# A decoder step on one core: the yo product moved from the first to the last place of each output run, B's transposes moved next to C·Bᵀ

## The chip, the cores and the metric

The kernel runs on one core of one Trainium2 chip, in a single launch. The metric is the device time of one execution in microseconds (us); lower is better.

## The reference

One inference step of a one-layer decoder trunk, for a prompt of 256 tokens and 8 sample requests of 4 tokens each (288 columns together). The core of what the change touches is the second head group of the mixer, a Mamba-2 chunked scan:

```python
proj = h @ lp['w_in']
u_pool, z, xbc, dt_raw = jnp.split(proj, ...)
pool_out = pool_mixer(u_pool, ...)
...
CB = jnp.einsum('bclgn,bcsgn->bclsg', Cm, Bm)
y_diag = jnp.einsum('bclsg,bclsgr,bcsgrp->bclgrp', CB, Lm, xdt)
...
y_off = jnp.einsum('bclgn,bcgrpn,bclgr->bclgrp', Cm, h_starts, jnp.exp(cs))
y = (y_diag + y_off).reshape((b, nc * q) + xdt.shape[3:])[:, :L]
...
y = y + d_skip * xs
y = rmsnorm(y * jax.nn.silu(z), norm_g)
...
mix = jnp.concatenate([pool_out, ssd_out], axis=-1) @ lp['w_out']
x = x + g1 * mix
...
x = x + g2 * ffn_out
```

Widths: model 2048, pooling mixer 512 (4 groups of 128), scan 1536 (24 heads of 64, in 4 groups of 6), state 128. Around it stand adaLN modulation from a 2048 x 12288 weight, RMSNorms and a gated MLP. Inputs and outputs are float32.

## The kernel before

Everything is held transposed: features on 128 partitions, 288 token columns. A large projection splits each float32 weight tile of 128x1024 into a rounded high part and a low part, and adds three products per 128x128 block: high by high, high by low, low by high (`mm3`, L304 to L306). For each such tile, called a half here (two for each block of 128 output rows), SP loads the raw tile (L271), ACT casts it into a `whi` slot (L290) and DVE subtracts into a `wlo` slot (L292). There are two slots of each kind in this stage: the cast of a half waits until TensorE is through with the half before the last.

The stage in question runs from about 236 to 395 us. Its outer loop goes over 16 halves of the `uz` projection (blocks 10 to 15, then 1 and 0; `project_units`). Between the pairs of blocks, a chain of generators (`back`) is pulled one step at a time: the convolution of each scan group (`conv_group`) and the scan itself (`ssd_group`, four groups). After the uz halves come the halves of the out projection (`out_units`), `mm_out` for the scan features and `mm_outp` for the four pooling groups.

One call of `ssd_group(g)` yields these steps: the transposes of x into tokens (`xt`, L788) with `xdt` and `xde` on DVE; the transposes of B (`bt`, L795, copied by ACT at L796); C·Bᵀ (`cb`, L802); the chunk states (`s`, L814, L821) and the product of the 8 sample states with C (`yo`, L834); then three pairs of heads t = 0, 1, 2. For each pair `decays(t)` broadcasts the cumulated decays by matmul (`cse`, L852), makes `e` on ACT (L857 to L859) and multiplies it on DVE with the C·Bᵀ block (`e`, L860) and with C (`ec`, L861). `outputs(t)` adds up the pair's output in one PSUM bank, `y`: six lines of short matmuls of 64 output rows by 128 or 32 columns, and a product with `yo` (L868) of 128 rows by 32 columns for the state part of the samples. DVE then adds the skip (L881) and multiplies with the gate (L885); ACT squares and POOL sums the squares (`ssq`).

Other work stands between these on the same engines. The modulation weights come in visits: four raw tiles of 512 KB into four own slots (`rawa`), 16 short matmuls (L406), and at once the loads of the next visit. The pooling groups (`pool_units`) build windowed sums on DVE (`pp`, `pq`, `pout`) and take one matmul each (L940). After the scan, `ysum` (L242) sums the squares over partitions, ACT and DVE turn the sums into 1/root (L248, L249), and `pbrstdy` (L255) spreads the result. The operand of the out projection is split like a weight, into `mixh` on ACT and `mixl` on DVE (L1127 and L1128, 12 of each).

All engines work in order. The order on each is not written out by hand in this stage. It is made when the program is built: a scheduler takes the instructions in the order written, with priorities for some, and places each when its inputs, its slot and its engine are free by its own cost model. PSUM banks for short-lived results (`aux`) are four, in turn. So a product that is written in another place can move other instructions on every engine.

Of the kernel before, what the change touches and what calls it, by code (L numbers as in the profile page):

```python
# [18 lines left out]
P = 128  # L19
D = 2048  # L20
KT = D // P
NP = 256
NB, NL = 8, 4
NS = NB * NL
N = NP + NS
# [139 lines left out]
def kernel(ctx: ExitStack, tc, ins, outs):  # L165
    nc = tc.nc
# [13 lines left out]
    def aux(name):  # L180
        return px.tile([P, 512], F32, tag="aux", name=name)
# [10 lines left out]
    seli = vec[:, K_SEL:K_SEL + 32]  # L192
# [345 lines left out]
    for q in range(4):  # L538
        t = mx.tile([P, 4, N], F32, tag="blk", name=f"xa{q}", bufs=4)
# [226 lines left out]
    def bc64(ap):  # L766
        return ap.unsqueeze(2).to_broadcast([ap.shape[0], HG, 64])

    def heads(ap):
        return ap.rearrange("p (h q) -> p h q", h=HG)  # L770

    def ssd_group(g):
# [10 lines left out]
        xdt = kp.tile([P, 3, G6], F32, tag="hmod", name=f"xdt{g}", bufs=2)  # L783
        xde = kp.tile([P, 3, G6], F32, tag="hmod", name=f"xde{g}", bufs=2)
        for c in range(3):
# [3 lines left out]
            nc.vector.tensor_tensor(heads(xdt[:, c, :]), heads(pt[:, :G6]), bc64(dt[:, c, hs]), ALU.mult)  # L789
            nc.vector.tensor_tensor(heads(xde[:, c, :]), heads(pt[:, :G6]), bc64(dtr["dtde"][:, c, hs]), ALU.mult)  # L790
        yield
        bt = sx[0].tile([P, 3, P], F32, tag="bt", name=f"bt{g}")
        pt = aux(f"bt{g}")
        for c in range(3):
            nc.tensor.transpose(pt[:, c * P:(c + 1) * P], toks(3, c), ident)  # L795
        nc.scalar.copy(bt.rearrange("p c n -> p (c n)"), pt[:, 0:3 * P])  # L796

        yield
        pcb = aux(f"cb{g}")
        for c in range(3):  # L800
            n = min(P, N - c * P)
# [35 lines left out]
        yo = sx[0].tile([P, G6], F32, tag="yo", name=f"yo{g}")  # L837
# [26 lines left out]
        def outputs(t, e, ec):  # L864
            assert (g, t) in zdone
            pq = aux(f"y{g}_{t}")
            rows = [slice(0, 64), slice(64, P)]
            nc.tensor.matmul(pq[:, NP:N], yo[:, P * t:P * t + P], seli, start=True, stop=False)  # L868
            for i, r in enumerate(rows):
                f = slice(64 * (2 * t + i), 64 * (2 * t + i) + 64)  # L870
                f = slice(64 * (2 * t + i), 64 * (2 * t + i) + 64)
                nc.tensor.matmul(pq[r, NP:N], xdt[:, 2, f], e[:, i, NP:N], start=False, stop=True)
            for i, r in enumerate(rows):
                f = slice(64 * (2 * t + i), 64 * (2 * t + i) + 64)
                nc.tensor.matmul(pq[r, 0:P], xdt[:, 0, f], e[:, i, 0:P], start=True, stop=True)
            for i, r in enumerate(rows):
                f = slice(64 * (2 * t + i), 64 * (2 * t + i) + 64)
                nc.tensor.matmul(pq[r, P:NP], xdt[:, 1, f], e[:, i, P:NP], start=True, stop=False)
                nc.tensor.matmul(pq[r, P:NP], s1[:, f], ec[:, i, :], start=False, stop=True)
            yt = cf[:, t, 0:N]  # L880
            nc.vector.scalar_tensor_tensor(out=yt, in0=yt,  # L881
                                           scalar=vec[:, V_D + 3 * g + t:V_D + 3 * g + t + 1],
                                           in1=pq[:, :N], op0=ALU.mult, op1=ALU.add)
            zt = zy[g][:, t, :]
            nc.vector.tensor_tensor(zt, zt, yt, ALU.mult)  # L885
            sq = kp.tile([P, N], F32, tag="xsq", name=f"ysq{g}_{t}", bufs=2)
            nc.scalar.activation(sq, zt, AF.Square)
            if g + t == 0:
                nc.gpsimd.tensor_copy(ssq, sq)
            else:  # L890
                nc.gpsimd.tensor_tensor(ssq, ssq, sq, ALU.add)
# [4 lines left out]
        yield  # L896
        dec.append(decays(1))
        outputs(0, *dec[0])
        yield
        dec.append(decays(2))  # L900
        outputs(1, *dec[1])
        yield
        outputs(2, *dec[2])
        yield

# [55 lines left out]
    with in_order(*(e.engine for e in (nc.tensor, nc.scalar, nc.vector))):  # L961
# [3 lines left out]
        for q in range(4):  # L965
# [5 lines left out]
            for i in range(4):  # L971
                nc.tensor.matmul(ssum[32 * i:32 * i + 32, :N], ones[:, 0:32], sq[:, i, :],
                                 start=(q == 0), stop=(q == 3), tile_position=(0, 32 * i))
# [54 lines left out]
    def take(gn, n):  # L1028
        for _ in range(n):
            next(gn)  # L1030
            yield

    ssd3 = ssd_group(3)
    back = chain(conv0, h0s(0), zip2(ssd_group(0), conv_group(1)), h0s(1),
                 zip2(ssd_group(1), conv_group(2)), h0s(2), zip2(ssd_group(2), conv_group(3)), h0s(3),
                 zip2(take(ssd3, TK), chain(pool_units(UEARLY[0]), pool_units(UEARLY[1]))))
    credit = {}
# [506 lines left out]
```

## Time and profile before

| what | value |
|---|---|
| time, median of 3 runs | 1345.85 us (1345.23 to 1345.96) |
| the profiled execution | 1344.82 us |
| its span in the trace | 1343.0 us, mean granted TensorE clock 0.998 |
| TensorE weight loads (PEld), busy | 1245.8 us |
| VectorE (DVE) busy | 823.3 us |
| ScalarE (ACT) busy | 578.4 us |
| GpSimd (POOL) busy | 221.3 us |

A line of the profile names the source line, the engine, the operation, the tile written, the tiles read and the shape. "busy" is the time in which an instruction of the engine was in work; matmuls overlap, so the distance between the starts of two matmuls is less than the duration of one. Waits are put down to the instruction that came last. The line numbers are those of the kernel before.

### The profile page before, as it was taken

The numbers are of one execution on the slowest core, as the hardware profiler recorded it, in microseconds if no ns is written. First come the engines' busy times: TensorE is split into PE (matmuls) and PEld (weight loads), VectorE is DVE, ScalarE is ACT, GpSimd is POOL, SyncE is SP. The second block draws the span as 40 slices with busy tenths as digits, with TensorE's granted clock in tenths as the row PEclk, the third lists the DMA queues.
The fourth block names the chain that finished last, engine by engine and source line by source line (L and its number), as shares of the span: only waits on it lengthen the run. The fifth ranks groups of instructions, "written<-read, shape, count | busy, mean of one in ns | idle before, by whom it ended". The sixth has DMA issues, their size and how long they took to land.

```text
span 1343.0 us, 26201 instructions
## 1 busy us (share of the span) xinstructions
PE 1328.6 (99%) x10517; PEld 1245.8 (93%) x10517; DVE 823.3 (61%) x1384; ACT 578.4 (43%) x912; POOL 221.3 (16%) x447
## 2 busy tenths in 40 slices
PE   9999999999999999999999999999999999999997
PEld 7899988776789889989999999999999999999997
DVE  5675569878765478555565455665655556666543
ACT  5343244677733335433433333434433334443442
POOL 0000012123122222102121001222210021122221
PEclk9999999999999999999999999999999999999999
DMA  9999778888898877776455555555555555555541
GB/s 372 405 371 376 275 266 303 312 303 314 299 397 331 309 255 263 277 273 226 169 194 168 169 175 183 204 184 200 185 164 167 186 192 192 193 197 195 179 132 71
DMA packets 97482, 323.19 MB, mean 241 GB/s; under 512 B 10768, under 2 KB 19920, under 8 KB 97360
## 3 DMA queue, kind: packets, MB, share of 16 engines
q1 hardware_dynamic: 93456, 310.72, 65.0%
q0 software_dynamic: 3184, 9.69, 2.0%
q8 instruction: 82, 1.34, 0.4%
q10 hardware_dynamic: 720, 1.11, 0.3%
q14 instruction: 40, 0.33, 0.1%
HBM read 309.78 MB, written 10.39 MB: 238 GB/s over the span
## 4 chain that ended last, share of the span: by engine, by line
PE 94%; DMA 4%; DVE 1%; ACT 0%; issue 0%; SPq 0%; POOL 0%; DVEq 0%
PE mm_down L305 7%; PE mm_down L304 7%; PE mm_down L306 7%; PE mm_val L305 6%; PE mm_gate L304 6%; PE mm_gate L305 6%; PE mm_val L306 6%; PE mm_gate L306 6%; PE mm_val L304 6%; PE xbc L304 4%; PE xbc L305 4%; PE xbc L306 4%; PE adap L406 4%; DMA raw_adap<-wflat 3%; PE adag L373 2%; PE mm_out L304 2%
## 5 line engine op out<-in xcount | busy, mean ns | idle before, releaser
L305 PE MATMUL mm_down<-al,whi_down 128*128 128x288 f32 x688 | 202.5, 294 | 0.0
L304 PE MATMUL mm_down<-ah,whi_down 128*128 128x288 f32 x688 | 202.4, 294 | 0.0
L306 PE MATMUL mm_down<-ah,wlo_down 128*128 128x288 f32 x688 | 202.0, 294 | 0.0
L305 PE MATMUL mm_val<-h2l,whi_val 128*128 128x288 f32 x640 | 189.1, 296 | 0.0
L305 PE MATMUL mm_gate<-h2l,whi_gate 128*128 128x288 f32 x640 | 189.0, 295 | 0.0
L304 PE MATMUL mm_gate<-h2h,whi_gate 128*128 128x288 f32 x640 | 188.7, 295 | 0.0
L306 PE MATMUL mm_val<-h2h,wlo_val 128*128 128x288 f32 x640 | 188.4, 294 | 0.0
L306 PE MATMUL mm_gate<-h2h,wlo_gate 128*128 128x288 f32 x640 | 188.3, 294 | 0.0
L304 PE MATMUL mm_val<-h2h,whi_val 128*128 128x288 f32 x640 | 188.0, 294 | 0.0
L292 DVE TENSOR_TENSOR wlo_gate<-raw_gate,whi_gate 128x1024 fp32r<-128x1024 f32 x80 | 98.6, 1232 | 132.7 <-ACT whi_gate L290 130.5
L292 DVE TENSOR_TENSOR wlo_down<-raw_down,whi_down 128x1024 fp32r<-128x1024 f32 x96 | 108.1, 1126 | 116.8 <-ACT whi_down L290 115.9
L290 ACT CAST whi_down<-raw_down 128x1024 fp32r<-128x1024 f32 x96 | 92.4, 962 | 166.8 <-PE mm_down L305 119.2
L290 ACT CAST whi_gate<-raw_gate 128x1024 fp32r<-128x1024 f32 x80 | 84.0, 1051 | 158.2 <-PE mm_gate L305 75.9
L290 ACT CAST whi_val<-raw_val 128x1024 fp32r<-128x1024 f32 x80 | 84.1, 1051 | 128.3 <-issue 113.6
L304 PE MATMUL xbc<-h1h,whi_xbc 128*128 128x288 f32 x448 | 133.1, 300 | 0.8 <-ACT h1h L491 0.7
L305 PE MATMUL xbc<-h1l,whi_xbc 128*128 128x288 f32 x448 | 132.3, 296 | 0.0
L306 PE MATMUL xbc<-h1h,wlo_xbc 128*128 128x288 f32 x448 | 130.1, 295 | 0.0
L304 PEld LDWEIGHTS mm_down<-ah,whi_down 128*128 128x128 f32 x688 | 129.2, 188 | 0.0
L305 PEld LDWEIGHTS mm_down<-al,whi_down 128*128 128x128 f32 x688 | 129.1, 188 | 0.0
L306 PEld LDWEIGHTS mm_down<-ah,wlo_down 128*128 128x128 f32 x688 | 129.0, 188 | 0.0
L304 PEld LDWEIGHTS mm_gate<-h2h,whi_gate 128*128 128x128 f32 x640 | 120.3, 188 | 5.0 <-ACT ah L1307 4.2
L306 PEld LDWEIGHTS mm_gate<-h2h,wlo_gate 128*128 128x128 f32 x640 | 120.5, 188 | 0.0
(335 smaller groups left out, 2978.5 us busy)
## 6 DMA issues: line engine op xcount, KB each, us to landing
raw_adap<-wflat SPq DMA_DIRECT2D x128, 512.0 KB, 6.2
raw_gate<-wflat SPq DMA_DIRECT2D x80, 512.0 KB, 3.6
raw_val<-wflat SPq DMA_DIRECT2D x80, 512.0 KB, 3.5
raw_ada<-wflat SPq DMA_DIRECT2D x64, 512.0 KB, 9.6
raw_xbc<-wflat SPq DMA_DIRECT2D x50, 512.0 KB, 9.7
raw_down<-wflat SPq DMA_DIRECT2D x48, 512.0 KB, 3.5
raw_out<-wflat SPq DMA_DIRECT2D x32, 512.0 KB, 7.4
raw_down<-wflat SPq DMA_DIRECT2D x32, 384.0 KB, 3.6
```

Of the source, the lines that this page charges most:

```text
L290: yield nc.scalar.copy(hi[:, :n], raw[:, a:a + n])
L292: yield hi, lo, nc.vector.tensor_tensor(lo[:, :n], raw[:, a:a + n], hi[:, :n].bitcast(F32), ALU.subtract)
L304: nc.tensor.matmul(ps, whi[:, w], bh, start=first, stop=False)
L305: nc.tensor.matmul(ps, whi[:, w], bl, start=False, stop=False)
L306: nc.tensor.matmul(ps, wlo[:, w], bh, start=False, stop=last)
L373: i = nc.tensor.matmul(ps[32 * j:32 * j + 32, :nb], sc_c[:, ck, :], raw[:, c:c + nb], start=q0 + n == 0, stop=q0 + AQ[gi] >= nq and n + 1 ...
L406: i = nc.tensor.matmul(ps[32 * j:32 * j + 32, :], sc_c[:, k, :], raw[:, 512 * (j % 2):512 * (j % 2) + 512], start=not begun and k == step - 1,
```

## The change

It moves two things within `ssd_group` and adds no instruction: TensorE has 9152 rows before and after (a row can stand for several equal instructions).

```diff
         yield
+        yield
         bt = sx[0].tile([P, 3, P], F32, tag="bt", name=f"bt{g}")
         pt = aux(f"bt{g}")
         for c in range(3):
             nc.tensor.transpose(pt[:, c * P:(c + 1) * P], toks(3, c), ident)
         nc.scalar.copy(bt.rearrange("p c n -> p (c n)"), pt[:, 0:3 * P])
-
-        yield
         pcb = aux(f"cb{g}")
...
             pq = aux(f"y{g}_{t}")
             rows = [slice(0, 64), slice(64, P)]
-            nc.tensor.matmul(pq[:, NP:N], yo[:, P * t:P * t + P], seli, start=True, stop=False)
-            for i, r in enumerate(rows):
...
-                nc.tensor.matmul(pq[r, NP:N], xdt[:, 2, f], e[:, i, NP:N], start=False, stop=True)
             for i, r in enumerate(rows):
                 f = slice(64 * (2 * t + i), 64 * (2 * t + i) + 64)
                 nc.tensor.matmul(pq[r, 0:P], xdt[:, 0, f], e[:, i, 0:P], start=True, stop=True)
...
+            for i, r in enumerate(rows):
+                f = slice(64 * (2 * t + i), 64 * (2 * t + i) + 64)
+                nc.tensor.matmul(pq[r, NP:N], xdt[:, 2, f], e[:, i, NP:N], start=True, stop=False)
+            nc.tensor.matmul(pq[:, NP:N], yo[:, P * t:P * t + P], seli, start=False, stop=True)
```

In the orders below, line numbers of the changed kernel are one or two lower or a few higher than those of the kernel before. The first place is group 1. On TensorE the yo products of its pairs 1 and 2 stood before among the matmuls of uz, far ahead of the runs to which they belong:

```order
L306 MATMUL mm_uz_12_3531<-h1h12_130,wlo_uz_12_1_3648 128x288
L304 MATMUL mm_uz_12_3531<-h1h13_131,whi_uz_12_1_3646 128x288
L868 MATMUL y1_1_3629<-vec_70,yo1_3484 128x32
L868 MATMUL y1_2_3656<-vec_70,yo1_3484 128x32
L305 MATMUL mm_uz_12_3531<-h1l13_147,whi_uz_12_1_3646 128x288
```

Now each stands at the end of its run, and the run of pair 2 stands ahead of the modulation visit, which in the order before came earlier (its first row is row 1726 before and row 1817 now):

```order
L305 MATMUL mm_uz_14_3931<-h1l14_148,whi_uz_14_1_4059 128x288
L306 MATMUL mm_uz_14_3931<-h1h14_132,wlo_uz_14_1_4061 128x288
L869 MATMUL y1_2_3656<-e1_2_3612,xdt1_3343 64x128 x2
L872 MATMUL y1_2_3656<-e1_2_3612,xdt1_3343 64x128
L873 MATMUL y1_2_3656<-ec1_2_3613,s1_1_3460 64x128
L872 MATMUL y1_2_3656<-e1_2_3612,xdt1_3343 64x128
L873 MATMUL y1_2_3656<-ec1_2_3613,s1_1_3460 64x128
L876 MATMUL y1_2_3656<-e1_2_3612,xdt1_3343 64x32 x2
L877 MATMUL y1_2_3656<-vec_70,yo1_3484 128x32
L338 MATMUL adat_p2_3677<-early_69,asb_p2_3510 128x128 x4
L406 MATMUL adap3_3683<-raw_adap_3_1_1_3550,sc_c_84 32x512 x2
```

Between the runs of pairs 0 and 1 of this group 46 matmuls of uz stand now, between those of pairs 1 and 2 68. On DVE, three low halves now stand ahead of the `e` of pair 2; before, the low half uz_14_0 came after it:

```order
L292 TENSOR_TENSOR wlo_uz_14_0_3936<-raw_uz_14_0_3932,whi_uz_14_0_3934 128x1024
L292 TENSOR_TENSOR wlo_uz_14_1_4061<-raw_uz_14_1_4057,whi_uz_14_1_4059 128x1024
L860 TENSOR_TENSOR ec1_2_3613<-ec1_2_3613,cf1_2987 128x256
L292 TENSOR_TENSOR wlo_uz_15_0_4144<-raw_uz_15_0_4140,whi_uz_15_0_4142 128x1024
L859 TENSOR_TENSOR e1_2_3612<-e1_2_3612,cb1_3434 128x576
```

The second place is the first half of the out projection. TensorE reaches its last block in this order now, where the matmul of pooling group 1 has come behind the product with `mixl11` (before, it stood 17 matmuls ahead of that product):

```order
L305 MATMUL mm_out_0_4626<-mixl10_4596,whi_out_0_0_4556 128x288
L306 MATMUL mm_out_0_4626<-mixh10_4580,wlo_out_0_0_4558 128x288
L304 MATMUL mm_out_0_4626<-mixh11_4581,whi_out_0_0_4556 128x288
L305 MATMUL mm_out_0_4626<-mixl11_4597,whi_out_0_0_4556 128x288
L938 MATMUL pool1_4527<-pout_4105,poolw_152 128x288
L306 MATMUL mm_out_0_4626<-mixh11_4581,wlo_out_0_0_4558 128x288
```

On DVE `mixl11` stood ahead of the low half out_0_1 before:

```order
L1128 SCALAR_TENSOR_TENSOR mixl10_4596<-zy2_3363,vec_70,mixh10_4580 128x288
L934 TENSOR_TENSOR pout_4111<-pout_4111,upp_115 128x16
L1128 SCALAR_TENSOR_TENSOR mixl11_4597<-zy2_3363,vec_70,mixh11_4581 128x288
L1128 SCALAR_TENSOR_TENSOR mixl12_4598<-zy2_3363,vec_70,mixh12_4582 128x288
L292 TENSOR_TENSOR wlo_out_0_1_4564<-raw_out_0_1_4560,whi_out_0_1_4562 128x1024
```

Now that low half and six instructions of the pooling groups stand between `mixl10` and `mixl11`:

```order
L1126 SCALAR_TENSOR_TENSOR mixl10_4596<-zy2_3363,vec_70,mixh10_4580 128x288
L921 TENSOR_TENSOR pp1_0_4448<-upp_115 128x270
L292 TENSOR_TENSOR wlo_out_0_1_4564<-raw_out_0_1_4560,whi_out_0_1_4562 128x1024
L921 TENSOR_TENSOR pp1_1_4452<-pp1_0_4448 128x268
L922 TENSOR_TENSOR pq0_0_4551<-ups_116 128x8x18
L928 SCALAR_TENSOR_TENSOR pout_4105<-pp1_1_4452,upp_115 128x256
L921 TENSOR_TENSOR pp0_0_4550<-upp_115 128x270
L931 TENSOR_TENSOR pout_4105<-pp1_1_4452,vec_70 128x16
L1126 SCALAR_TENSOR_TENSOR mixl11_4597<-zy2_3363,vec_70,mixh11_4581 128x288
L932 TENSOR_TENSOR pout_4105<-pout_4105,upp_115 128x16
```

What also moved: between the last run of the scan and the out projection TensorE had 27 matmuls of uz and one visit; now it has 12 matmuls of uz.

The third place is the sum of squares, on TensorE. Before, 15 matmuls of `mm_out` stood between `ysum` and `pbrstdy`, the first of them here:

```order
L338 MATMUL adat_p3_4530<-early_69,asb_p3_4519 128x128 x4
L940 MATMUL pool0_4644<-pout_4111,poolw_152 128x288
L242 MATMUL ysum_4667<-ones_71,ssq_156 128x1 x3
L305 MATMUL mm_out_0_4626<-mixl15_4601,whi_out_0_1_4562 128x288
L306 MATMUL mm_out_0_4626<-mixh15_4585,wlo_out_0_1_4564 128x288
```

Now `pbrstdy` follows `ysum` directly:

```order
L306 MATMUL mm_out_1_4729<-mixh15_4585,wlo_out_1_1_4765 128x288
L338 MATMUL adat_p3_4530<-early_69,asb_p3_4519 128x128 x4
L938 MATMUL pool0_4644<-pout_4105,poolw_152 128x288
L242 MATMUL ysum_4667<-ones_71,ssq_156 128x1 x3
L255 MATMUL pbrstdy_4674<-early_69,r3rstdy_4671 128x128 x2
L255 MATMUL pbrstdy_4674<-early_69,r3rstdy_4671 128x32
L304 MATMUL mm_outp_0_4627<-mixh3_4573,whi_out_0_1_4562 128x288
```

All twelve `mm_out` blocks of the second output block run ahead of that now, while the half out_0_1 stays in its slot for its `mm_outp` blocks; so the half out_1_1 takes the slot of out_1_0, the half just before it. From the fifth output block on, the order of TensorE is the old one again.

More of the change, by code (lines that the diff above doesn't have):

```diff
@@ L867, in outputs @@
             rows = [slice(0, 64), slice(64, P)]
-            nc.tensor.matmul(pq[:, NP:N], yo[:, P * t:P * t + P], seli, start=True, stop=False)
-            for i, r in enumerate(rows):
-                f = slice(64 * (2 * t + i), 64 * (2 * t + i) + 64)
-                f = slice(64 * (2 * t + i), 64 * (2 * t + i) + 64)
-                nc.tensor.matmul(pq[r, NP:N], xdt[:, 2, f], e[:, i, NP:N], start=False, stop=True)
             for i, r in enumerate(rows):
```

## The prediction

> **What bounds the kernel now.** First the page, engines and chain:
>
> ```profile
> PE 1328.6 (99%) x10517; PEld 1245.8 (93%) x10517; DVE 823.3 (61%) x1384; ACT 578.4 (43%) x912; POOL 221.3 (16%) x447
> PE 94%; DMA 4%; DVE 1%; ACT 0%; issue 0%; SPq 0%; POOL 0%; DVEq 0%
> ```
>
> TensorE is busy for 1328.6 of 1343.0 us, so time is won only by making its work cheaper and lost by every wait that it takes on. The change touches only the scan and what follows, so next the table by windows of 25 us there (after the width of the window: PE, PEld, DVE, ACT, POOL busy, the granted clock, the DMA engines' share):
>
> ```profile
> 250.00:275.00 25.00, 25.00 (x214) 18.93 (x214) 19.38 (x39) 21.09 (x47) 3.69 (x8) 1.00 0.88 325
> 275.00:300.00 25.00, 24.86 (x217) 19.29 (x217) 17.07 (x29) 20.16 (x44) 5.72 (x7) 1.00 0.86 300
> 300.00:325.00 25.00, 24.40 (x205) 17.22 (x203) 21.87 (x41) 21.83 (x48) 6.79 (x11) 1.00 0.85 321
> 325.00:350.00 25.00, 23.96 (x194) 17.57 (x191) 18.36 (x34) 15.84 (x35) 5.37 (x8) 1.00 0.80 299
> 350.00:375.00 25.00, 24.73 (x201) 20.36 (x201) 19.78 (x46) 16.40 (x37) 5.17 (x11) 1.00 0.88 320
> ```
>
> TensorE idles 2.05 us of these 125 (125 less the sum 122.95). That is all that a better order could recover here. DVE and ACT are busy for 63 to 87% in these rows, so they have little slack if TensorE's order asks for their results earlier. The table of TensorE's waits names the idle time:
>
> ```profile
> PE adap L406 <- DMA raw_adap<-wflat: 0.8, 2, 0.6
> PE pool L940 <- DVE pout L934: 0.6, 1, 0.6
> PE y L872 <- DVE e L860: 0.4, 1, 0.4
> ```
>
> A wait costs more than its idle time, since the matmul before it still counts as busy (0.29 us against a distance of 0.13): with some six waits of 0.16 more, I put the cost before at 2.05 + 0.96 = 3.0 us.
>
> **The yo product itself.** The timeline has both arrangements. Alone among uz matmuls (first four rows), directly behind a run (next four), and a run without it (last four):
>
> ```profile
> 348.81 0.30 PE L305 MATMUL mm_uz<-h1l,whi_uz 128*128 128x288 f32 x1
> 348.95 0.30 PE L868 MATMUL y<-vec,yo 128*128 128x32 f32 x2
> 349.09 0.38 PE L306 MATMUL mm_uz<-h1h,wlo_uz 128*128 128x288 f32 x1
> 349.30 0.30 PE L304 MATMUL mm_uz<-h1h,whi_uz 128*128 128x288 f32 x1
> ...
> 317.75 0.44 PE L879 MATMUL y<-ec,s 128*64 128x128 f32 x4
> 318.12 0.41 PE L868 MATMUL y<-vec,yo 128*128 128x32 f32 x2
> 318.36 0.38 PE L305 MATMUL mm_uz<-h1l,whi_uz 128*128 128x288 f32 x1
> 318.58 0.29 PE L306 MATMUL mm_uz<-h1h,wlo_uz 128*128 128x288 f32 x1
> ...
> 326.85 0.44 PE L879 MATMUL y<-ec,s 128*64 128x128 f32 x4
> 327.21 0.40 PE L304 MATMUL mm_uz<-h1h,whi_uz 128*128 128x288 f32 x1
> 327.45 0.29 PE L305 MATMUL mm_uz<-h1l,whi_uz 128*128 128x288 f32 x1
> 327.58 0.30 PE L306 MATMUL mm_uz<-h1h,wlo_uz 128*128 128x288 f32 x1
> ```
>
> Alone: 0.49 us from the matmul ahead to the second one behind, against 0.26 for two plain steps (349.30 to 348.81; a plain step is 327.58 to 327.45, 0.13), so 0.23. Behind the run: 0.83 from the run's last line to the second matmul, against 0.60 without yo, so again 0.23. The move is worth nothing by itself, except where the lone product also waited. For that, and for B's transposes sharing one entry and one exit with C·Bᵀ, I take −0.5 us. Bounds: 0, and −1.8 if each of 12 runs saved the 0.11 by which the step after a run's exit (0.24) exceeds a plain one and each of 4 groups as much again.
>
> **What the new order makes late.** The durations on DVE and ACT come from the groups in this stretch:
>
> ```profile
> L290 ACT CAST whi_out<-raw_out 128x1024 fp32r<-128x1024 f32 x12 | 12.4, 1045 | 5.8 <-PE mm_outp L305 2.4 <-DMA raw_out<-wflat 2.0 <-PE mm_out L305 0.8
> L292 DVE TENSOR_TENSOR wlo_uz<-raw_uz,whi_uz 128x1024 fp32r<-128x1024 f32 x16 | 19.5, 1218 | 3.6 <-ACT whi_uz L290 3.6
> L860 DVE TENSOR_TENSOR e<-e,cb 128x576 f32<-128x576 f32 x12 | 9.0, 752 | 0.3
> L861 DVE TENSOR_TENSOR ec<-ec,cf 128x256 f32<-128x256 f32 x12 | 6.0, 499 | 4.6 <-ACT ec L858 4.6
> L881 DVE SCALAR_TENSOR_TENSOR cf<-cf,vec,y 128x288 f32<-128x288 f32 x12 | 6.1, 512 | 8.0 <-PE y L879 8.0
> L1128 DVE SCALAR_TENSOR_TENSOR mixl<-zy,vec,mixh 128x288 fp32r<-128x288 f32 x12 | 6.5, 558 | 0.0
> L923 DVE TENSOR_TENSOR pp<-pp 128x268 f32<-128x268 f32 (+2 forms) x6 | 4.4, 737 | 0.6 <-POOL ssq L891 0.5
> L930 DVE SCALAR_TENSOR_TENSOR pout<-pp,upp 128x256 f32<-128x256 f32 x4 | 1.7, 422 | 0.1
> ```
>
> A uz cast costs what an out cast does, 1.05.
>
> *Group 1, 1.1 us.* The low half uz_15_0 cannot be written until TensorE has finished uz_14_0, cast 1.05 and handed over (about 0.1): it ends 2.4 us after that half's last product with its high part, and the `e` of pair 2, now queued behind it, at 3.2. TensorE has 22 uz matmuls to put there, 2.9 us at 0.132, and then waits 0.4; with the drain 0.5. Pair 1 is alike, two low halves ahead of its `e`: cast and low half 2.4, `ec` 0.5 and `e` 0.75 give 3.7 against 25 matmuls and a little, 3.3, so 0.4 to 0.5. Another 0.1 for a low half. Bounds 0 and 2.5.
>
> *The other nine runs, C·Bᵀ, the first pooling matmuls, 1.3.* Nothing there is clearly better or worse off than before, where the named waits came to 0.4 and 0.6 plus drains. Bounds 0 and 3.
>
> *The first out half, 3.0.* This is the largest term. The operand of the out projection comes from DVE, 0.56 a block. After the last run of the scan TensorE has 12 uz matmuls (1.6 us) where it had 27 and a visit (3.6 + 1.9). On DVE out_0_1's low half now stands ahead of `mixl11`. It needs the slot of the last uz half, then a cast: it could start 1.2 us after the last uz matmul, ends at 2.4, and the six instructions to the end of `mixl11` bring 5.1 (`pp` 0.74, `pout` 0.42, `mixl` 0.56, and three smaller ones that I estimate at 1.0 together, each below `pp`). Until then TensorE has 22 matmuls, 2.9 us, so it waits 2.2. DVE may also come to that low half late: behind the last run it has 0.51 for the skip, as much for the gate, four `mixl` and a window sum, some 3.7 us with the hand-over, where 2.8 are free. With that 0.8 the wait is 3.0. It ends on the pooling product behind one more DVE instruction. Bounds: 0.5 if DVE finds gaps for its pooling work, 3.8.
>
> *Half out_1_1, 1.2.* It takes the slot of the half just before it, so 1.05 of cast and its hand-over lie bare on TensorE; the low half is covered by a visit. Nothing can stand in between, so bounds are 1.0 and 1.4.
>
> *The sum of squares, 0.7.* The timeline before:
>
> ```profile
> 369.82 0.72 PE L242 MATMUL ysum<-ones,ssq 128*128 128x1 f32 x6
> 370.58 0.26 ACT L248 ACTIVATE r3rstdy<-ysum,epst 128x3 f32<-128x3 f32 x1 [0.54 <-PE ysum L242]
> 370.88 0.18 DVE L249 RECIPROCAL r3rstdy<-r3rstdy 128x3 f32<-128x3 f32 x1 [0.34 <-ACT r3rstdy L248]
> 372.46 0.75 PE L255 MATMUL pbrstdy<-early,r3rstdy 128*128 128x128 f32 x6
> ```
>
> From `ysum` to `pbrstdy` TensorE did 15 other matmuls. From the end of `ysum` (370.54) to that of the reciprocal (371.06) it is 0.52, and I add 0.2 for the hand-over back to TensorE (as between the end at ACT, 370.84, and DVE's start, and as much again). Now TensorE waits for all of it. Bounds 0.5 and 1.0 (DVE busy).
>
> *The visits, 0.4.* A visit's last load can land 1.1 + 1.3 (four issues in turn) + 6.2 us after its start, 8.6, by these rows:
>
> ```profile
> 334.14 1.92 PE L406 MATMUL adap<-raw_adap,sc_c 128*32 128x512 f32 x16
> 335.23 1.75 SPq L271 DMA_DIRECT2D raw_adap<-wflat  x4
> raw_adap<-wflat SPq DMA_DIRECT2D x128, 512.0 KB, 6.2
> ```
>
> Since the first visit of part 3 moved back by 91 rows, the eight distances from there to the first visit of part 4 now hold only some 72 us of TensorE's work (its rows at these prices). By counted rows, only one is short: from chunks 12 and 13 to 14 and 15 TensorE has 37 matmuls and the visit, 7.0 us, and 1.2 of wait for out_1_1: 0.4 is missing. Bounds 0 and the second rival.
>
> **Sum:** 1.1 + 1.3 + 3.0 + 1.2 + 0.7 + 0.4 = 7.7 of waits, less 3.0 of old ones, less 0.5: +4.2. On the profiled execution, 1344.82, that is 1349.0. That execution lay 1.03 under the median of 1345.85, so the forecast for a median is 1345.85 + 4.2 = **1350.0 us** (slower by 0.3%).
>
> **Rivals.**
>
> *DVE keeps ahead (faster).* If DVE does its pooling work early, in gaps that open as TensorE's runs come later, the first out half does not wait, and group 1 neither. What speaks for it: DVE shows 3 to 8 idle us in each window. Then only the waits without any cover stay, 1.2 + 0.7; with the old 3.0 gone and the upper saving of 1.8, 1345.85 + 1.9 − 4.8 = 1342.95. It decides once the wait at the first out half is under 0.5 us. Against it: DVE works in order, and `mixl11` stands behind a low half whose slot TensorE itself frees last.
>
> *The visits become the bound.* Before, a visit's loads behind other loads took longer:
>
> ```profile
> 366.13 1.99 PE adap L406 x16
> 368.60 8.33 DMA raw_adap<-wflat
> 376.97 1.92 PE adap L406 x16
> ```
>
> That is 10.8 from visit to visit, with the visit waiting for the load. If each of the eight distances needs 10.8, they take 86 in place of 72; the 5 us of other waits in them are hidden by it, so 9 come on top of the sum, 1359, and 4.5 if half of them do: 1354.5. Against it: the DMA engines have room (0.80 to 0.88 of their time in the windows), and the out loads mostly follow a visit's loads in SP's order. The Trainium skill, "DMA: Bandwidth & Descriptors", section "Issuing engines are not separate DMA queues", says that all transfers run on the same 16 engines and interleave, whoever issued them; by it an out load issued right behind a visit's four would slow them too, and the distance of 10.8 is the rule, not 8.6. The rows here bear it out for the visits with two out loads near, not for the others.
>
> *No change.* The waits fall by half, since each wait on TensorE gives DVE time for the next: 3.9 less 3.5, 1346.2.
>
> **How the numbers follow.** Forecast 0.52, no change 0.22, DVE keeps ahead 0.16, visits 0.10. A measurement of this kernel tells about 0.2% (2.7 us) from no change. Slower by more: most of the first, all of the last, 0.62. Within: 0.24. Faster: most of the rival, 0.14. The forecast's own bounds (first out half 0.5 to 3.8, group 1 and the nine runs 0 to 5.5) are 1346 to 1354; eight in ten reach from 1343.8 to 1354.8.
>
> **What would show it.** TensorE's waits should name `mixl` L1126 or `pout` as what the first out half waited for, some 3 us in one or two pieces; a wait of about 1 on ACT's `whi_out`; one of 0.5 to 0.7 at `pbrstdy` on DVE's reciprocal; two of about 0.3 to 0.5 at the `y` runs of group 1. Between the runs' last line and the second matmul behind the yo there should be 0.83 us. I am wrong if the first out half does not wait, or if the visits wait for `raw_adap` by more than 2 us together.

## The result, and the profile after

| | before | after |
|---|---|---|
| median of the runs side by side | 1345.73 us (1345.11 to 1347.90) | 1354.26 us (1352.64 to 1355.70) |
| the profiled execution | 1344.82 us | 1354.68 us |
| its span | 1343.0 us | 1352.9 us |

The changed kernel takes 1.0061 times as long (95% interval 1.0048 to 1.0074): 8.5 us more by the medians, 9.9 between the two profiled executions. Forecast was 4.2 more, within a range that ends at 1354.8.

The page of the changed kernel, engines and chain:

```profile
PE 1331.1 (98%) x10517; PEld 1247.7 (92%) x10517; DVE 826.2 (61%) x1384; ACT 579.0 (43%) x912; POOL 220.4 (16%) x447
PE 91%; DMA 4%; DVE 2%; issue 2%; ACT 1%; POOL 0%; SPq 0%; DVEq 0%; POOLq 0%; ACTq 0%
```

TensorE has the same 10517 matmuls and is busy for only 2.5 us more; the rest, 7.4, is idle time. The table by windows shows where (columns as in the prediction):

```profile
275.00:300.00 25.00, 25.00 (x209) 21.69 (x208) 16.58 (x26) 21.53 (x44) 5.09 (x6) 1.00 0.87 312
300.00:325.00 25.00, 23.69 (x195) 17.23 (x195) 22.48 (x43) 19.36 (x46) 5.81 (x9) 1.00 0.82 294
325.00:350.00 25.00, 23.88 (x189) 16.16 (x191) 17.54 (x34) 16.14 (x33) 7.40 (x9) 1.00 0.61 223
350.00:375.00 25.00, 21.68 (x176) 16.60 (x176) 19.26 (x43) 14.55 (x38) 7.23 (x11) 0.93 0.81 291
375.00:400.00 25.00, 21.55 (x163) 17.79 (x162) 13.09 (x25) 9.90 (x14) 2.87 (x8) 1.00 0.91 347
```

From 275 to 300 TensorE never idles. From 350 to 400 TensorE idles 6.8 us, and the clock is 0.93 in one window. The DMA engines, at 0.80 between 325 and 350 before, are at 0.61 there. TensorE's waits between 236 and 420 (in all, times, longest):

```profile
PE mm_out L305 <- DVE mixl L1126: 3.3, 1, 3.3
PE adap L406 <- DMA raw_adap<-wflat: 2.6, 3, 1.3
PE pool L938 <- DVE pout L932: 1.1, 1, 1.1
PE mm_out L304 <- ACT whi_out L290: 1.0, 1, 1.0
PE y L869 <- DVE e L859: 0.7, 1, 0.7
PE cse L851 <- DVE yo L837: 0.6, 1, 0.6
PE pbrstdy L255 <- DVE r3rstdy L249: 0.6, 1, 0.6
```

Read by itself, this table confirms the forecast: its largest row is the wait on `mixl` at the first out half, and most others are the ones named. The experiments show that it misleads. The modulation is worked off in numbered parts of eight visits each; when a part's sums are complete, ACT copies them out (L332) and TensorE transposes them (`adat_p`, L338). What counts is what stands in the chain of waits, from the last visits of part 3 to the first of part 4:

```profile
368.56 3.16 PE adap L406 x16
...
372.10 7.15 DMA raw_adap<-wflat
...
379.30 2.00 PE adap L406 x16
...
381.30 0.37 SPq L271
...
381.72 7.71 DMA raw_adap<-wflat
...
389.47 1.92 PE adap L406 x16
```

Here one visit hands over to the next: a visit's last slot is free when the visit ends, its load is issued, lands 7 to 8 us later, and the next visit can begin. TensorE waited for the loads by 1.30 and 0.58 us in these two places. The forecast gave the visits 0.4. All waits for visits' loads come to 2.6 us in the table, over the 2 that the prediction named as a sign of being wrong; one of them, 0.8, lies at 256 us, ahead of part 3.

And this chain begins late. The timeline of the changed kernel where part 3's first visit starts, first ACT, then TensorE:

```profile
281.66 0.58 ACT L332 COPY asb_p<-adap 128x512 f32<-128x512 f32 x1
...
304.50 0.41 PE L877 MATMUL y<-vec,yo 128*128 128x32 f32 x2
304.74 0.63 PE L338 MATMUL adat_p<-early,asb_p 128*128 128x128 f32 x4
305.31 1.07 PE L406 MATMUL adap<-raw_adap,sc_c 128*32 128x512 f32 x8
```

and of the kernel before:

```profile
280.37 0.59 ACT L332 COPY asb_p<-adap 128x512 f32<-128x512 f32 x1 [0.64 <-PE adap L406]
...
291.69 0.60 PE L338 MATMUL adat_p<-early,asb_p 128*128 128x128 f32 x4
292.22 1.07 PE L406 MATMUL adap<-raw_adap,sc_c 128*32 128x512 f32 x8
```

Part 2's sums leave for ACT at about the same time in both. Their transposes (`adat_p`) and with them part 3's first visit come 13.1 us later now, directly behind the run of group 1's pair 2.

### The profile page after: what moved, and what is told of

It is laid out like the page before. It is cut to its first block, busy times and chain, and to the rows that moved or that the text cites. A ratio compares the mean times of both kernels' runs of the same rounds, so it can differ in the third digit from the quotient of the medians.

```text
span 1352.9 us, 26213 instructions
## 1 busy us (share of the span) xinstructions
PE 1331.1 (98%) x10517; PEld 1247.7 (92%) x10517; DVE 826.2 (61%) x1384; ACT 579.0 (43%) x912; POOL 220.4 (16%) x447
## 4 chain that ended last, share of the span: by engine, by line
PE 91%; DMA 4%; DVE 2%; issue 2%; ACT 1%; POOL 0%; SPq 0%; DVEq 0%; POOLq 0%; ACTq 0%
PE mm_down L305 7%; PE mm_down L304 7%; PE mm_down L306 7%; PE mm_val L305 6%; PE mm_gate L304 6%; PE mm_gate L305 6%; PE mm_val L306 6%; PE mm_gate L306 6%; PE mm_val L304 6%; PE xbc L304 4%; PE xbc L305 4%; PE xbc L306 4%; PE adap L406 4%; PE adag L373 2%; PE mm_out L304 2%; DMA raw_adap<-wflat 2%
```

## The experiments

The theory of the first four is that of the forecast: results of DVE and ACT that come late behind the new order make the loss. They led to another one, the chain of visits, and the other eight tell the two apart. From the fifth run on the expectations call the chain theory 1 and the late results theory 2.

**One part at a time.** The yo product alone, with B's transposes as before (the lines against the changed kernel):

```diff
         yield
-        yield
         bt = sx[0].tile([P, 3, P], F32, tag="bt", name=f"bt{g}")
...
+        yield
         pcb = aux(f"cb{g}")
```

> Only the yo product moved to the end of each run; B's transposes stay one step ahead of C·Bᵀ as before. Theory (the loss is made of TensorE's new waits, which the new order brings): this order also has the long stretches of uz between the pairs of groups 1 and 2 and the late visits, but mixl11 stands ahead of the low half out_0_1 and 30 uz matmuls lie between the last run and the out projection, so the 3.3 us wait and the slow clock behind it are missing. Slower than before by 2 to 5 us, 1348 to 1351, TensorE's idle time in 225 to 400 us some 4 to 6. Rival (the yo product itself is dearer at the end of a run): about the same loss as the whole change, 1354, with TensorE's busy time up and not its idle time.

Measured: 1349.27 us, ratio 1.0029 (1.0018 to 1.0041). The size is as expected, the cause is not: there is no wait on `mixl`, and three quarters of the idle time are visits waiting for loads:

```profile
PE adap L406 <- DMA raw_adap<-wflat: 3.7, 3, 1.7
PE mm_out L306 <- DVE wlo_out L292: 0.9, 2, 0.7
```

In this trace six of the eight visits that follow part 3's first one start within 0.05 us of the landing of their last load, so here the chain of visits sets the pace almost throughout.

The kernel before with B's transposes moved and the yo product as it was:

> Only B's transposes moved next to C·Bᵀ; the yo product opens the group as before. Theory: the scheduler still places the yo products early and claims the bank early, the visits stay about 10 us apart, and the out projection starts as before: within 0.2% of before, 1343.5 to 1348.5, with some 2 to 3 us of idle TensorE in 225 to 400 us. Rival (sharing the step with C·Bᵀ is what makes things late): 3 us or more slower.

Measured: 1346.76, ratio 1.0008 (0.9999 to 1.0017), as expected. The two parts alone make 3.7 and 1.2 us against the kernel before in the same comparison (1345.57), less together than the whole change. Part 3's first visit starts at 301.86 with the first part, 293.57 with the second, 305.31 with both.

**The long wait split.** One short product with a pooling buffer, into columns that nothing reads, stands in the middle of the wait for `mixl11` in the changed kernel:

```diff
+                    nc.tensor.matmul(pz[:, :N], hi[:, w], xhi[0][MIXK[k]], start=False, stop=False)
+                    nc.tensor.matmul(pz[:, N:N + 128].rearrange("p (b l) -> p b l", l=16), poolw[:, 0, :],
+                                     mid[0][:, :, 3:19], start=False, stop=False, skip_group_check=True)
+                    nc.tensor.matmul(pz[:, :N], hi[:, w], xlo[0][MIXK[k]], start=False, stop=False)
```

> The changed kernel with one added matmul (pq of pooling group 0 by a pooling weight, 128 columns, into unused columns of the mm_out bank), which stands on TensorE ahead of the product with mixl11 and waits for DVE's pq0_0, about in the middle of the 3.3 us wait. All other rows of all engines are as in the changed kernel. Theory (a wait this long lets the clock fall to half for some 3.5 us, and the stretched visit behind it issues its loads later): the wait stays 3.3 us in two pieces of about 2 and 1, the granted clock stays 1.00 in 365 to 375 us, the visit behind it takes 1.9 in place of 3.15, and the time is 1.5 to 3 us below the changed kernel's 1354.3: 1351.3 to 1352.8. Rival (the clock's fall has another cause, or the slow visit is one of data): the visit still takes about 3 us, and the time stays 1354.3.

Measured: 1355.09, ratio 1.0072 (1.0059 to 1.0085): a miss. In the profiled execution, the fastest of the five (1353.33), it did what it was made for, the wait in two pieces (TensorE's waits):

```profile
PE mm_out L1143 <- DVE pq L923: 2.1, 1, 2.1
...
PE mm_out L1145 <- DVE mixl L1129: 0.7, 1, 0.7
```

and the clock at 1.00 (window of 5 us; TensorE's busy time, clock, DMA share):

```profile
365.00:370.00 5.00, 2.89 (x19) 1.00 0.68 228
```

The other four executions had a mean clock of 0.994 to 0.997 against 0.998 and took 1354.44 to 1357.21, no less than the changed kernel (1352.64 to 1355.70); where the clock fell in them no trace shows.

**The long wait taken away.** In the changed kernel, operand blocks 10 and 11 get priority:

```diff
-            nc.scalar.activation(xhi[0][k], zy[g][:, t, :], AF.Identity, scale=gv)
-            nc.vector.scalar_tensor_tensor(out=xlo[0][k], in0=zy[g][:, t, :], scalar=gv,
...
+            with tc.high_priority() if k in (10, 11) else nullcontext():
+                nc.scalar.activation(xhi[0][k], zy[g][:, t, :], AF.Identity, scale=gv)
+                nc.vector.scalar_tensor_tensor(out=xlo[0][k], in0=zy[g][:, t, :], scalar=gv,
...
```

> The changed kernel with mixh and mixl of blocks 10 and 11 given priority, so that DVE makes mixl11 ahead of the low half out_0_1; orders are otherwise as in the changed kernel but for 14 rows of TensorE and 16 of DVE around the first out half. Theory (DVE's order made the 3.3 us wait): that wait goes; in its place about 1 for the cast of the next half and about 1 for mixl12, neither long enough for the clock to fall. 2 to 4.5 us below the changed kernel: 1349.8 to 1352.3. Rival (the wait stands on the slow sum of squares of POOL or on loads, whatever the order on DVE): wait and time as in the changed kernel.

Measured: 1353.49, ratio 1.0063 (1.0051 to 1.0076), against 1.0061 for the change itself: a miss, and the one that brought the theory of late results down. The 3.3 us are gone from the waits, but others have grown:

```profile
PE adap L406 <- DMA raw_adap<-wflat: 3.2, 4, 1.1
PE mm_out L304 <- ACT whi_out L290: 1.9, 2, 1.0
...
PE mm_out L305 <- DVE mixl L1127: 0.9, 1, 0.9
```

Part 4's first visit starts at 388.27, where it started at 389.47 with the wait and at 376.97 before the change. The trace of the changed kernel says why so little was to be won there: the stretch between two visits that holds the 3.3 us wait is 12.59 us long, and the loads for the second visit had landed 11.16 us after the first began, so that without the wait it could have come 1.43 us earlier at most. That led to the theory of the chain. In every kernel of this study that has this visit at TensorE rows 2176 to 2179, the span from its start to the end is 963.4 or 963.5 us (966.0 to 966.6 where 20 to 24 more matmuls stand behind it). So a kernel's whole difference is decided by when that visit starts, and the question is what holds it.

**The first visit of part 3 put first.** In the changed kernel, part 2's transposes go behind part 3's first visit:

```diff
-            if end:
-                ada_end(*end)
-                end = None
             if k0 == 0:
                 ps = pa.tile([P, 512], F32, tag="ada", name=f"adap{part}")
             whole(ps, ahead, step, True, begun)
             ahead.clear()
+            if end:
+                ada_end(*end)
+                end = None
```

> The changed kernel with one step moved: the transposes of part 2's adaLN sums are put behind part 3's first visit instead of ahead of it, so that this visit no longer waits for a bank that the y runs hold. On TensorE it then stands at row 1707 (changed kernel 1817, before 1726) and part 4's first visit at 2156 (2177, 2157). With it the last two pooled operand blocks' low parts also come ahead of the first out projection's second low half. Theory 1, the chain of visits sets the loss (each visit's loads start only at the visit, so eight distances of 10.2 to 10.8 us from a first visit that is 13 us late): the first visit comes at 288 to 292 us, part 4's first at 375 to 379 as before the change, and the median is 1345 to 1349.5, most of the 8.5 us gone. Theory 2, the late results of VectorE and ScalarE behind the new order are the loss and the visits only follow: only the 2.6 us on record as waiting for loads and the 0.8 us that the run with the operand first gained can go, so 1351 to 1354.

Measured: 1346.08, ratio 1.0008 (1.0000 to 1.0017). The first visit starts at 289.82, part 4's first at 378.48. Nearly the whole loss is gone, with the yo product at the end of its runs, as the chain would have it. All waits that TensorE's table still lists in the stretch:

```profile
PE adap L406 <- DMA raw_adap<-wflat: 1.5, 3, 0.6
PE pool L938 <- DVE pout L932: 0.8, 2, 0.6
PE cse L851 <- DVE cb L804: 0.5, 1, 0.5
```

As the order is made anew, `mixl11` and `mixl12` also came ahead of the low half out_0_1 here, so this run alone could still be read by the theory of late results.

**The opposite.** The kernel before, with part 3's first visit put off:

```diff
             if end:
+                for _ in range(6):
+                    yield
                 ada_end(*end)
```

> The kernel before, its yo product at the head of each run and its transposes apart as they were, with one step later: part 3's first visit is put off by six steps of its sequence, and stands at TensorE row 1797 instead of 1726; all eight visits and the first of part 4 (row 2178 instead of 2157) follow. On VectorE the operand's blocks 10 to 12 still stand ahead of the first out projection's second low half, as before the change. Theory 1 (chain of visits): the first visit comes at about 301, eight distances of 10.2 to 10.6 bring part 4's first to 383 to 386 where before it was 377, 2.7 of that is the work of 21 more rows ahead of it, and the median is 1348 to 1352. Theory 2 (late results behind the new order): the order of the runs is the old one, so the time stays within 1345 to 1347.

Measured: 1354.72, ratio 1.0069 (1.0056 to 1.0083), the loss of the whole change without any of it. That is above the range of either theory. The visit came at 305.31, not 301, to the hundredth where the change puts it; the eight distances behind it, 83.91 us, are as expected, and part 4's first came at 389.22. Five of the eight visits after it start within 0.05 us of the landing of their last load. Yet the waits are others, and at the first out half there is none on `mixl`:

```profile
PE adap L406 <- DMA raw_adap<-wflat: 3.4, 4, 1.4
PE pbrstdy L255 <- DVE r3rstdy L249: 2.0, 1, 2.0
PE mm_out L304 <- ACT whi_out L290: 1.0, 1, 1.0
PE adat_p L338 <- ACT asb_p L332: 0.9, 1, 0.9
PE mm_out L306 <- DVE wlo_out L292: 0.7, 1, 0.7
```

**The dose.** The same with 8 in place of 6:

> As the run with the visit late in the kernel before, put off by eight steps in place of six: part 3's first visit at TensorE row 1847 (1797 there), part 4's first at 2178 as there. Theory 1 (chain of visits): 50 more rows of 0.13 us ahead of it bring the first visit from 305.3 to about 312; the eight distances take 83 to 84 us again, so part 4's first visit comes at 395 to 396, and behind it lie 963.4 us as in all runs that have it at rows 2177 to 2179: a span of 1358.5 to 1359.5 and a median of 1358.5 to 1361. Theory 2 (late results behind the runs): nothing but the visits is moved further, so the time stays at that run's 1354.7, within 1 us.

Measured: 1361.69 (1359.56 to 1363.35), ratio 1.0119 (1.0105 to 1.0133). First visit at 313.50, part 4's first at 394.28, span 1357.8: a little under what was expected for the span, the median a little over. The chain shows a distance from one visit to the next that no other work of TensorE fills, so that it idles 8.06 us:

```profile
373.34 1.99 PE adap L406 x16
375.33 0.01 issue
375.34 1.21 SPq L271
376.55 0.05 issue
376.60 6.68 DMA raw_adap<-wflat
383.28 0.04 issue
383.32 3.71 PE adap L406 x16
```

That is 9.98 us, where the forecast had 8.6: the last load goes out 3.26 us after the visit's start (2.4 in the forecast) and takes 6.68 (6.2).

**The same step in the kernels that were not slow.** The kernel before, and the second part alone, with part 2's transposes behind the first visit:

> The kernel before with the same step moved as in the changed one: part 2's transposes behind part 3's first visit, which then stands at TensorE row 1704 instead of 1726. Theory 1: before the change the visits wait for loads by 0.8 us in all, so at most about 1 us is to be won here: 1344 to 1346.5. Theory 2: no difference beyond what a measurement tells, the same range; this run tells the theories apart only together with the two others, and shows what the moved step is worth by itself.

> Only the second part of the change (B's transposes in one step with C B^T), yo product at the head of each run, with part 2's transposes behind part 3's first visit. Without this step the second part alone was 1346.76 with 1.2 us of waits for visits' loads and 1.3 for the pooling operand. Theory 1: the visits' waits go, 1344.5 to 1346.5. Theory 2: it stays at 1346 to 1348.

Measured: 1347.12, ratio 1.0014 (1.0006 to 1.0022), and 1346.31, ratio 1.0008 (0.9999 to 1.0016). Where the chain does not bind, an earlier start wins nothing: the first is even 0.1% slower than before and misses its range (other waits grew, 2.0 on `pout` and 1.1 on `yo`); the second is not told from its 1.0008 without the step.

**Both theories' cures together.** The changed kernel with the first visit first, and priority for all twelve gated operand blocks:

> The changed kernel with part 3's first visit freed (as in the run that did it alone, 1346.08) and, on top, the twelve gated operand blocks' casts and low parts of the out projection given priority. Theory 1: the chain of visits no longer binds there, and TensorE waits 2.9 us in all between 236 and 425, so at most 1 to 2 us are to be won: 1344 to 1346.5, no faster than the kernel before by more than can be told. Theory 2 (late results behind the new order are what costs): 1342 to 1344.5, faster than before.

Measured: 1346.82, ratio 1.0013 (1.0004 to 1.0022), 0.3 above the range for the chain, and 2.3 above that for late results. With the chain free, results of DVE made earlier win nothing.

**Why the visit is late.** The four shared PSUM banks are handed out in the order in which the program is written, and the transposes of part 2 come there behind the y run of pair 2. In the kernel before, that run opened its bank with the lone yo product (row 1702, the visit at 1726); now it opens only when its `e` is there (row 1809, the visit at 1817). In the changed kernel, part 2's transposes get the bank of their own sums instead:

```diff
-        pt = aux("adat_" + name)
+        pt = pa.tile([P, 512], F32, tag="ada", name="adat_p2") if name == "p2" else aux("adat_" + name)
```

> The changed kernel with one line altered: part 2's transposes go into the bank that part 2's own sums have just left, not into one of the four banks that the y runs, C B^T and the pooling products share; their place in the program is as in the changed kernel, ahead of part 3's first visit. They then stand at TensorE row 1697 and that visit at 1705 (changed kernel 1816 and 1817). If the late first visit is put off by the shared banks and nothing else, the first visit comes at 288 to 293 us in place of 305.3, part 4's first at 377 to 382, and the median is 1344.5 to 1348, about as with the visit put first (1346.08). If the visit is late for another reason (its loads, or the sums' copy on ScalarE), it waits there on TensorE and the time stays above 1351.

Measured: 1344.87 (1343.40 to 1346.21), ratio 0.9995 (0.9987 to 1.0004): the loss is gone with one line. The first visit starts at 287.96, part 4's first at 378.65. The only wait that TensorE's table still lists in the stretch:

```profile
PE pool L938 <- DVE pout L932: 1.6, 2, 0.8
```

The same line in the kernel before prices the change itself:

> The kernel before (yo product at the head of each run, transposes of B apart) with the same line altered as in the run with the own bank: part 2's transposes in the bank that its sums have left. They stand at TensorE row 1697, part 3's first visit at 1705 (before 1725 and 1726). Against the changed kernel with that line (1344.87, no wait for a visit's load left) this prices the change itself with the visits out of the way. If the change's own worth is about nothing, as its matmuls are the same in number and form, the two lie within 2 us: 1344 to 1347. If the late results behind the changed order cost the 4 to 5 us that were summed for them even with the visits freed, this run comes out at 1340 to 1341. If the move saves the 0.5 to 1.8 us put on it, it comes out at 1345.4 to 1346.7.

Measured: 1345.66, ratio 1.0002 (0.9993 to 1.0011). Against the kernel before, the two stand at −0.34 and +0.32 us by the medians; the intervals overlap, so that the change by itself wins some 0.7 us at best guess, and that cannot be told from nothing. It is not the 1340 to 1341 that late results would have given. No kernel here beats the one before by more than its interval.

## Why the prediction was right in sign and short in size

| kernel | part 3's first visit | part 4's first visit | between | span |
|---|---|---|---|---|
| before | 292.22 | 376.97 | 84.75 | 1343.0 |
| after | 305.31 | 389.47 | 84.16 | 1352.9 |
| yo product alone | 301.86 | 384.56 | 82.70 | 1348.0 |
| operand first | 304.69 | 388.27 | 83.58 | 1351.7 |
| before, visit late | 305.31 | 389.22 | 83.91 | 1352.7 |
| before, visit later | 313.50 | 394.28 | 80.78 | 1357.8 |
| visit first | 289.82 | 378.48 | 88.66 | 1344.6 |
| own bank | 287.96 | 378.65 | 90.69 | 1342.1 |

(Starts from the timelines, in us.) A distance is the time from the start of one visit to that of the next. The five kernels here with a first visit after 300 take 80.8 to 84.2 for the eight distances, 10.1 to 10.5 on the mean (single ones 8.93 to 12.59), whichever waits TensorE's table names; those with an early visit have 88 to 91 and wait little. The kernel before is between: 84.75, but filled with work, as TensorE idles only 2.2 us in the whole stretch.

*The sign and the range.* Slower, within the range, near its upper end. The profiled execution would have been forecast at 1349.0; it took 1354.68. The forecast's own bounds end at 1354, just under the measured 1354.26; their lower end is added up wrongly, for the terms at their lower bounds (0.5 for the first out half, nothing for group 1 and the nine runs) give 2.8 less 3.5, so 1345.2 and not 1346. The sign came in part by luck: the waits from which the forecast had it do come, but the kernel before with a late visit loses as much without the largest of them.

*The failed step: the visits, 0.4.* The prediction had the essential row counts, a first visit 91 rows later and 72 us of work left for eight distances. What it had wrong is the price of a link, that is the time from a visit's start until the last of the four loads that it issues has landed: 8.6 us, with the median of all such loads. In the trace of the changed kernel the eight links take 8.38 to 11.16 us, 9.70 on the mean; the last load goes out 2.73 after the visit's start (2.4 in the forecast) and takes 6.97 (6.2). For the four loads of the visit at 305.31 and of that at 355.90 the trace gives, from issue to landing:

```profile
DMA to landing us min/median/max: 3.5/4.8/6.1
...
DMA to landing us min/median/max: 6.1/6.5/7.9
```

Eight links of 8.6 are 68.8 us and would hide behind the work; the measured eight are 77.6 and do not. With these landings the chain alone would let part 4's first visit start at 382.9. Without it that visit would, by estimate, stand at 379.6: where it stood before, plus 2.6 us for some 20 matmuls that are ahead of it now. So 3.3 us of the 9.9 are the links themselves. The other 6.6 are the time by which visits started after their loads had landed, 0.36 to 1.43 us in six of the eight distances: there TensorE's own work and the waits of the table below fill the distance. That a late first visit makes the loss is shown, by the runs that move only this visit; how the loss divides between links and waits is worked out from this one trace and was not tried by a run of its own.

*The rival "the visits become the bound" was the case.* Its chance was 0.10. Its lower price, 1354.5, was met. Its reasoning was that links are 10.8; they are 9.70 on the mean, between the 8.6 of the forecast and the 10.8 of the rows quoted for the rival, and the other waits were hidden in part only. Of the rule of the Trainium skill weighed there ("DMA: Bandwidth & Descriptors", section "Issuing engines are not separate DMA queues"), the runs show no more than that links differ. The prediction's reading that two out loads near make the difference does not hold: in the kernel before, the visit at 334.14 had two out loads issued 2.9 and 3.6 us after its start, and its link was 9.08. That it is the sharing of the engines that makes a link longer was not tried.

*The other terms had about the right size and did not set the time.* From the idle list of the profiled execution, with 0.16 for the drain of each wait:

| term | forecast | measured |
|---|---|---|
| group 1 | 1.1 | 0.8 (one wait, not two) |
| other runs, C·Bᵀ, pooling | 1.3 | 2.1 (0.6 and 1.1, with drains) |
| first out half | 3.0 | 3.5 |
| half out_1_1 | 1.2 | 1.2 |
| `ysum` to `pbrstdy` | 0.7 | 0.7 |
| visits | 0.4 | 3.1 (2.2 of it in the eight distances) |

The waits stand where they were foreseen. But a wait inside a distance can win back no more than the time until the next visit's loads have landed: without the 3.3 us for `mixl` the total hardly moved, and the kernel before with a late visit lost as much by quite other waits. The measured terms add up to 11.4, less 3.0 of old waits 8.4, and with 1.2 for the clock 9.6 of 9.9: the sum closes, and still its terms are not causes of their own. In the runs with the visit freed hardly any of these waits is left, with the same order within the runs; that it is the visits, standing between the runs again, that cover them is a reading which no run tests.

*The yo product itself, and the shared step: −0.5.* With the bank out of the way the change is worth −0.7 us, not told from 0. That agrees with "nothing by itself". One sign came out otherwise: from the last line of a run to the second matmul behind the yo product it is 0.70 us (293.06 to 293.76 in the changed kernel's timeline), not 0.83; the last line now is a product of 32 columns.

*DVE keeps ahead; no change.* Neither came. "No change" is what the kernel does with the bank freed.

*Not foreseen: the clock,* 1.2 us on one visit and some more around it; see below.

## What to carry to other kernels

When a change moves a link of a chain that feeds itself (a transfer that starts only when the last one has been used), count the chain from its first link: the number of links times their measured mean, not times the median of one transfer, against the work that is left beside it. Here the difference, 9.70 against 8.6, turned a chain that would hide behind 72 us of work into one that does not. The table of waits names who came last, not what sets the end: if a wait taken away leaves the time as it was, look for the first instruction behind which all spans are equal, and ask what holds that one. And look at what the moved instruction opened, here a PSUM bank in a fixed turn: work that has nothing to do with it can stand behind it.

## What the runs showed of the hardware

The granted clock fell for a few us in places where TensorE had had little to do, and the matmuls then took nearly twice as long (up to 1059 ns for one of a visit, in place of 592). TensorE's busy time, clock and DMA share in windows of 5 us, in the changed kernel around the wait of 3.3 us:

```profile
360.00:365.00 5.00, 3.69 (x28) 1.00 0.97 375
365.00:370.00 5.00, 2.99 (x13) 0.76 0.72 238
370.00:375.00 5.00, 5.00 (x38) 0.90 0.76 262
```

The visit that began there took 3.16 us, others 1.92. With the operand first, where no wait just ahead of it was over 0.94 us (0.88 and 0.94), it fell as well:

```profile
365.00:370.00 5.00, 4.06 (x21) 0.66 0.77 237
```

And after the idle 8.06 us of the latest visit it was 0.50 in a whole window, with a visit of 3.71:

```profile
380.00:385.00 5.00, 1.68 (x8) 0.50 0.85 342
```

The Trainium skill, "TensorE: Matmul & The Clock Gate", section "HAM oscillation — how this bites in real kernels", puts it that gaps of TensorE over about 3.4 us bring the half clock. The runs agree for the 8.06, and go further: it also fell at 3.32, and with two short waits and few matmuls between them, while in one execution of the split wait (2.12 and 0.71) it stayed at 1.00. With the yo product alone, too, it stayed at 1.00 in a window of 5 us in which TensorE was busy for 3.32. What decides below 3.4 us was left open.
